# Scan's triangular inverses: substitution over 16x16 blocks, joined to 32x32 by small TensorE products

## The chip, the cores and the metric

One core of a Trainium2 chip. The metric is the device time of one execution in microseconds (us).

## The reference

A two-layer backbone over 512 latent and 256 context tokens of width 1024. Layer 0 mixes tokens by a gated MLP, layer 1 by a bidirectional RWKV-7 scan, and each layer ends in a mixture of experts. The change is in the scan of layer 1, which per direction and head (16 heads of 64) runs

```python
def _wkv_step(S, inp):
    r_t, w_t, k_t, v_t, a_t, b_t = inp
    sa = jnp.einsum('zbhvk,zbhk->zbhv', S, a_t)
    S = S * w_t[..., None, :] + sa[..., :, None] * b_t[..., None, :] + v_t[..., :, None] * k_t[..., None, :]
    return S, jnp.einsum('zbhvk,zbhk->zbhv', S, r_t)
```

first over the context, then over the latents. The kernel takes 64 tokens at a time. Within such a chunk the recurrence is a unit lower triangular system of 64x64 for each head, so each chunk and head needs the inverse of (I + L), with L strictly lower triangular.

## The kernel before

The scan stage (`Rwkv.wkv`) has 12 chunks in two directions, taken four at a time (two chunks of both directions) in six groups m = 0 to 5. Groups 0 and 1 are context, 2 to 5 latents. For a group there are three kinds of work:

- **prep_chunk** (four times a group) loads the chunk's keys and rates, scales them on VectorE (DVE) into `ZZ` and `BK`, lets TensorE (PE) form the attention blocks (`attend`, L1807) and transposes of `BK` (`turn`, L1828), and copies on ScalarE (ACT, L1816) the triangles L into `XT`.
- **invert** (once a group, for 4 chunks x 16 heads = 64 triangles, as 32 slots u of two) inverts. `gather` (L1852) transposes blocks so that each of the 128 partitions holds one 32x32 diagonal block. Forward substitution then runs on DVE: for each column j from 0 to 30 one product (L1856, into `subt`) and one subtraction (L1861, into `X`), each waiting for the one ahead. Two transposes bring the inverses back as `Dn` (L1881) and `Dt` (in the buffer of `Lp`, L1883). ACT places `Dt` in `XT` (`put`, L1865). PE then joins pairs of 32x32 to 64x64: `left` (L1896), an ACT copy with the sign turned (L1911), `right` (L1902), and an ACT copy into `XT` (L1916), all in two halves of 16 slots.
- **scan_step** (four a group) runs `read` (L1943), `solve` with the inverse (L1948), `update` (L1953) and, for latents, `outputs` (L1960, L1963) on PE; DVE (L1997) and GpSimd (POOL, L1998) bring the state on. Finished latents go through `finish` (DVE, and a transpose on PE, L2043).

The order on every engine is fixed when the program is built. Each `add` gives the planner (`Plan.run`) a step with an assumed cost, what it reads and what it writes. The planner takes the step that can start first by these costs, with the due times of `DUE` inside a small window. Buffers are rings: `X`, `Lp` and `Dn` have one each, the PSUM banks `p` three. Where the planner expects PE to stand idle ahead of a step that opens a bank, `Plan.fill` (L1146) issues products of the identity into that bank, about 0.8 of the expected idle time at 0.222 us each, and one in any case for the rings `p` and `y`:

```python
n = int(min(gap, FILLMAX) * FILL / 0.222) if gap >= FILLMIN else 0
for _ in range(max(n, XF if b.ring in XR else 0)):
    nc.tensor.matmul(q[:, 0:128], self.ident, self.ident, start=True, stop=True)
```

These fillers are real instructions: at run time they take their time whether or not PE would have waited. One f32 matmul is two records of the trace.

Of the kernel before, what the change touches and what calls it, by code (L numbers as in the profile page):

```python
# [17 lines left out]
P = 128  # L18
# [305 lines left out]
class Moe:  # L324
# [654 lines left out]
    def overflow(self, ep, ps, after):  # L979
# [5 lines left out]
        with tc.For_i(0, nv) as i:  # L985
# [57 lines left out]
            for g in after.groups:  # L1043
# [156 lines left out]
class Rwkv:  # L1200
# [474 lines left out]
    def consts(self, cp):  # L1675
        k = self.k
        nc = k.nc

        self.maskR = cp.tile([P, C], F32, name="maskR")
        self.maskY = [cp.tile([P, C], F32, name=f"maskY{z}") for z in range(2)]  # L1680
        for t, s in ((self.maskR, -1), (self.maskY[1], 1)):
            for h in range(2):
                nc.gpsimd.iota(t[64 * h:64 * h + 64, :], pattern=[[1, C]], base=0, channel_multiplier=s,
                               allow_small_or_imprecise_dtypes=True)
        nc.vector.tensor_scalar(self.maskY[0], self.maskR, 0.0, None, op0=ALU.is_ge)
        nc.vector.tensor_scalar(self.maskY[1], self.maskY[1], 63.0, None, op0=ALU.is_le)
# [146 lines left out]
    def invert(self, m):  # L1833


        add, nc = self.plan.add, self.k.nc
        self.plan.tag = "invert", 2 * m, 0
        g = m % 2
        XT = self.XT[:, g].rearrange("p c j t -> p (c j) t")
        Lk = [("L", g, i, n, p) for i in range(4) for n in range(2) for p in range(2)]  # L1840
        Lp, X, Dn, Dt = (self.buf(n, [P, 32, 32]) for n in ("Lp", "X", "Dn", "Lp"))

        def eye():
            nc.gpsimd.memset(X.t, 0.0)
# [26 lines left out]
        add("POOL", 1.8, eye, w=[(X, 0), (X, 1)])  # L1871
        add("DVE", 1.14, gather, r=Lk, w=[(Lp, 0)])
        for j in range(31):
            for e, (eng, w, a, b) in enumerate((("DVE", nc.vector, 0, min(j + 1, SPLIT)), ("POOL", nc.gpsimd, SPLIT, j + 1))):
                if a < b:
                    n = (31 - j) * (b - a)
                    c = 0.17 + n * 0.0021 if e else 0.07 + n / 960.0
                    t = self.buf(("subt", "subp")[e], [P, n], bufs=2)
                    add(eng, c, lambda w=w, t=t, j=j, a=a, b=b: times(w, t, j, a, b), r=[(X, e), (Lp, 0)], w=[t])
                    add(eng, c, lambda w=w, t=t, j=j, a=a, b=b: minus(w, t, j, a, b), r=[t], w=[(X, e)])  # L1880
        add("DVE", 1.14, lambda: nc.vector.transpose(Dn.t.rearrange("p u s -> p s u"), X.t.rearrange("p t s -> p s t")),  # L1881
            r=[(X, 0), (X, 1)], w=[(Dn, "1")])
        add("DVE", 1.14, lambda: nc.vector.transpose(Dt.t.rearrange("p u t -> p t u"), X.t), r=[(X, 0), (X, 1)], w=[Dt])  # L1883

        def put(b):
            add("ACT", 0.95, lambda: place(b), r=[Dt], w=[("XT", g, "diag", b)])

        for hf in range(2):
            us = range(16 * hf, 16 * hf + 16)
            q, q2 = self.bank([P, 16, 32]), self.bank([P, 16, 32])  # L1890
# [8 lines left out]
            def right(q=q2, us=us):  # L1899
                for u in us:  # L1900
                    for a, b in zip(fst, snd):
                        nc.tensor.matmul(q.t[a, u - us[0], :], Dn.t[b, u, :], XT[b, u, 32:64], start=True, stop=True,  # L1902
                                         tile_position=(b.start, a.start))

            self.plan.tag = "invert", 2 * m, 1
            add("PE", 0.9, left, r=[(Dn, "1")] + Lk, w=[q])
            if hf == 0:
                for b in (1, 3):
                    put(b)
            for p in range(2):  # L1910
                add("ACT", 0.48, lambda q=q, b=snd[p], us=us: nc.scalar.activation(Dn.t[b, us[0]:us[0] + 16, :], q.t[b], AF.Copy,  # L1911
                                                                                  scale=-1.0),
                    r=[q, (Dn, "1")], w=[(Dn, hf, p)])
            add("PE", 1.45, right, r=[(Dn, hf, 0), (Dn, hf, 1), ("XT", g, "diag", 1), ("XT", g, "diag", 3)], w=[q2])
            for p in range(2):
                add("ACT", 0.48, lambda q=q2, a=fst[p], us=us: nc.scalar.copy(XT[a, us[0]:us[0] + 16, 32:64], q.t[a]), r=[q2],  # L1916
                    w=[("XT", g, "off", hf, p)])
        for b in (0, 2):
            put(b)
        add("POOL", 1.8, blank, r=[(Lp, 0)], w=[("XT", g, "zero")])  # L1920

    def scan_step(self, h, z, c):
        add, nc = self.plan.add, self.k.nc
# [6 lines left out]
        s = self.sets.pop((z, c))  # L1930
        g, i = self.slot[z, c]
        Ti = self.XT[:, g, i]
        XTk = ([("XT", g, "off", i // 2, p) for p in range(2)] + [("XT", g, "diag", b) for b in range(4)] +
               [("XT", g, "zero")] + [("L", g, i, n, p) for n in range(2) for p in range(2)])
        SV = Buf(f"SV{z}", lambda: [self.sp.tile([P, KD, C], F32, name=f"SV{q}{z}", bufs=1) for q in range(2)], LATE)
        R, U, Sn, Y = self.bank([P, KD, C], "s3"), self.bank([P, KD, C], "s3"), self.bank([P, KD, C], "sn"), \
# [329 lines left out]
```

## Time and profile before

| | us |
|---|---|
| median of 3 runs (2615.51 to 2632.64) | 2625.8 |
| profiled execution | 2626.88 |
| its span | 2625.1 |
| scan stage in it, first gather to last write | 1554 to 2030 |
| share of the span that PE is busy | 91% |
| share that DVE is busy | 41% |
| share that ACT is busy | 28% |

Times in rows are us from the span's start. "Busy" of PE counts fillers too. [...]

### The profile page before, as it was taken

The page shows a single profiled execution, that of the slowest core. Times are in us where ns is not written, and L with a number is a line of the kernel's source. Part 1 is how long each engine was busy: PE and PEld are TensorE (multiplying, and loading weights), DVE is VectorE, ACT ScalarE, POOL GpSimd, SP SyncE. Part 2 cuts the span into 40 slices and gives each one's busy share as a digit, 9 for nine tenths or more (in the row PEclk, how much of TensorE's full clock was granted, in tenths as well). Part 3 has the DMA queues.
Part 4 walks back from the last instruction along what each step waited for, and adds up shares of the span by engine and source line. Part 5 has one row for each costly group of instructions (what it writes and reads, how often), then busy time and mean ns, then how long its engine had stood idle before and what let it go on. Part 6 is the DMA issues. An engine that isn't in the chain of part 4 may idle for free. (4 is left out here: it accounts for less than half of the span.)

```text
span 2625.1 us, 38933 instructions
## 1 busy us (share of the span) xinstructions
PE 2386.7 (91%) x15574; PEld 1514.6 (58%) x15574; DVE 1087.0 (41%) x2007; ACT 723.0 (28%) x1226; POOL 346.3 (13%) x306
## 2 busy tenths in 40 slices
PE   6999999997999999979979899889888799999985
PEld 2878997774334333346745488878787543333332
DVE  4334334444132111177655364887887511211113
ACT  3222213331000000036654345566544210000001
POOL 0000000003332222200012111211222110000000
PEclk8999999997999999988988699889999899999998
DMA  7135316558999999962256564533335699999995
GB/s 251 57 128 184 121 65 204 189 207 341 409 421 395 407 404 395 382 257 87 74 169 176 144 181 117 114 90 96 89 80 147 246 396 420 421 418 414 418 417 226
DMA packets 280077, 640.24 MB, mean 244 GB/s; under 512 B 131084, under 2 KB 156940, under 8 KB 229460
## 3 DMA queue, kind: packets, MB, share of 16 engines
q1 hardware_dynamic: 266548, 608.69, 63.0%
q0 software_dynamic: 11904, 23.77, 2.4%
q10 hardware_dynamic: 1440, 5.24, 0.5%
q8 instruction: 124, 2.03, 0.3%
q14 instruction: 61, 0.50, 0.1%
HBM read 580.65 MB, written 76.02 MB: 250 GB/s over the span
## 5 line engine op out<-in xcount | busy, mean ns | idle before, releaser
L935 PE MATMUL gu_ps<-e_raw,xT 128*64 128x512 f32 (+1 forms) x2048 | 587.4, 598 | 15.4 <-DMA e_raw<-moe_w_up 12.2
L935 PEld LDWEIGHTS gu_ps<-e_raw,xT 128*64 128x64 f32 (+1 forms) x2048 | 209.9, 149 | 372.7 <-issue 322.1
L891 PE MATMUL o_ps<-e_raw,hT 128*64 128x512 f32 (+1 forms) x1024 | 297.7, 603 | 5.0 <-ACT hT L867 5.0
L976 DVE TENSOR_TENSOR h_e<-gu_ps,h_e 128x512 f32<-128x512 f32 x39 | 27.0, 692 | 468.1 <-PE gu_ps L935 468.1
L891 PEld LDWEIGHTS o_ps<-e_raw,hT 128*64 128x64 f32 (+1 forms) x1024 | 104.7, 149 | 158.6 <-issue 144.4
L975 ACT ACTIVATE h_e<-gu_ps 128x512 f32<-128x512 f32 x39 | 23.3, 597 | 562.9 <-PE gu_ps L935 545.5
L1146 PE MATMUL p<-ident 128*128 128x128 f32 x892 | 139.9, 300 | 9.2 <-ACT BKt L1831 5.2
L1146 PEld LDWEIGHTS p<-ident 128*128 128x128 f32 x892 | 118.1, 204 | 21.7 <-ACT BKt L1831 7.2
L867 ACT COPY hT<-eT_ps 128x512 f32<-128x512 f32 x39 | 22.9, 586 | 355.6 <-PE eT_ps L861 355.6
L896 DVE SCALAR_TENSOR_TENSOR yo<-o_ps,wslot,gt_e 128x512 f32<-128x512 f32 x40 | 30.0, 751 | 182.2 <-issue 128.8
L826 POOL DMA_INDIRECT ybuf<-yo,idx x37 | 37.3, 1007 | 460.8 <-DVE yo L896 453.7
L73 PE MATMUL u_ps<-hh,w_hi 128*128 128x384 f32 x256 | 90.5, 353 | 4.9 <-ACT w_hi L66 4.9
L896 DVE SCALAR_TENSOR_TENSOR yo<-o_ps,wslot,gt2B 128x512 f32<-128x512 f32 x38 | 28.5, 750 | 158.2 <-PE o_ps L891 156.7
L812 POOL DMA_INDIRECT xg<-hbuf,idx x39 | 41.4, 1061 | 383.7 <-PE eT_ps L861 308.8
L74 PE MATMUL u_ps<-hl,w_hi 128*128 128x384 f32 x256 | 87.6, 342 | 0.0
L75 PE MATMUL u_ps<-hh,w_lo 128*128 128x384 f32 x256 | 86.3, 342 | 0.8 <-DVE w_lo L67 0.8
L67 DVE TENSOR_TENSOR w_lo<-w_raw,w_hi 128x1024 fp32r<-128x1024 f32 x56 | 67.9, 1222 | 38.1 <-ACT w_hi L66 37.4
L123 PE MATMUL ada_ps<-w_raw,cstat 128*32 128x512 f32 x384 | 62.8, 630 | 21.3 <-DMA w_raw<-ada_w 21.0
L73 PE MATMUL v_ps<-w_hi,hh 128*128 128x512 f32 x192 | 75.6, 406 | 3.9 <-ACT w_hi L66 3.9
L75 PE MATMUL v_ps<-w_hi,hl 128*128 128x512 f32 x192 | 75.7, 394 | 0.0
L74 PE MATMUL o_ps<-w_lo,gh 128*128 128x512 f32 x192 | 75.5, 395 | 0.0
L74 PE MATMUL v_ps<-w_lo,hh 128*128 128x512 f32 x192 | 75.5, 395 | 0.0
(562 smaller groups left out, 4415.1 us busy)
## 6 DMA issues: line engine op xcount, KB each, us to landing
e_raw<-moe_w_gate SPq DMA_DIRECT2D x128, 1024.0 KB, 19.8
e_raw<-moe_w_up SPq DMA_DIRECT2D x128, 1024.0 KB, 20.1
e_raw<-moe_w_down SPq DMA_DIRECT2D x128, 1024.0 KB, 19.8
w_raw<-ada_w SPq DMA_DIRECT2D x96, 512.0 KB, 6.4
w_raw<-ga_w_in SPq DMA_DIRECT2D x32, 512.0 KB, 6.5
Td<-c_st SPq DMA_DIRECT2D x64, 192.0 KB, 3.2
T<-Td SPq DMA_DIRECT2D x24, 512.0 KB, 4.9
ybuf<-zero_rows SPq DMA_DIRECT2D x20, 512.0 KB, 5.3
```

The source lines that it names most:

```text
L67: k.nc.vector.tensor_tensor(lo, src, hi.bitcast(F32), op=ALU.subtract)
L73: mm(out, a[0], b[0], start=start, stop=False)
L74: mm(out, a[0], b[1], start=False, stop=False)
L75: mm(out, a[1], b[0], start=False, stop=stop)
L123: nc.tensor.matmul(q[32 * g:32 * g + 32, :], k.cstat[:, j, :], w, start=(j < 4), stop=(j >= 4), tile_position=(0, 32 * g))
L812: k.nc.gpsimd.indirect_dma_start(out=xg[:], out_offset=None, in_=self.hbuf[:, :], in_offset=bass.IndirectOffsetOnAxis(ap=self.idx[:, 1, b: ...
L826: st = self.k.nc.gpsimd.indirect_dma_start(out=self.ybuf[:, :], out_offset=bass.IndirectOffsetOnAxis(ap=self.idx[:, 0, b:b + 1], axis=0), ...
L891: mm(o[hf][rows], hT[i][:, c, rows], self.raw[r, 4 + c // 2][:, f], start=c == 0, stop=c == 3)
L896: stt(yo[:, half(hf)], o[hf], self.wslot[:, u:u + 1], g[:, half(hf)], op0=ALU.mult, op1=ALU.mult)
L935: mm(q[gu][rows], xT[i][:, kk, rows], self.raw[r, 2 * gu + kk // 4][:, f], start=kk == 0, stop=kk == KD - 1)
L976: nc.vector.tensor_tensor(hv, u, hv, op=ALU.mult)
L1146: nc.tensor.matmul(q[:, 0:128], self.ident, self.ident, start=True, stop=True)
```

## The change

The diagonal blocks that DVE inverts become 16x16. One partition holds two of them (the two diagonal quarters of its 32x32 block), and one instruction works on both by a four-dimensional view, for columns 0 to 14. `X` and `Lp` get a row more (33 x 32), so that the two quarters lie a constant step apart. PE then joins 16x16 to 32x32 for each slot: `mid` multiplies the block with the inverse, ACT takes the result with a mask and the sign (`lower` is 0 or -1) into `Q` (in `X`'s buffer), `mid_n` makes the missing quarter of `Dn`, which DVE adds to it, and `mid_t` the missing quarter of `Dt`, which ACT places in `XT` (`between`). `left` and `right` are as before, but `left` now waits for the two additions and `right` for `between`. Some assumed costs are set anew (transposes 1.9 for 1.14, ACT copies 0.58 for 0.48, `left` 1.3 for 0.9).

```diff
-        def times(eng, t, j, a, b):
-            nr, nco = 31 - j, b - a
-            eng.tensor_tensor(t.t.rearrange("p (a b) -> p a b", a=nr), Lp.t[:, j + 1:, j:j + 1].to_broadcast([P, nr, nco]),
-                              X.t[:, j:j + 1, a:b].to_broadcast([P, nr, nco]), op=ALU.mult)
+        def times(t, j):
+            nr, nco = 15 - j, j + 1
+            nc.vector.tensor_tensor(
+                view(t, j), blocks(Lp)[:, :, 32 * (j + 1) + j:32 * 15 + j + 1:32][:, :, :, None].to_broadcast([P, 2, nr, nco]),
+                blocks(X)[:, :, 32 * j:32 * j + nco][:, :, None, :].to_broadcast([P, 2, nr, nco]), op=ALU.mult)
...
-        add("DVE", 1.14, gather, r=Lk, w=[(Lp, 0)])
-        for j in range(31):
...
+        add("DVE", 1.9, gather, r=Lk, w=[(Lp, 0)])
+        for j in range(15):
+            n = 2 * (15 - j) * (j + 1)
+            t = self.buf("subt", [P, n], bufs=2)
+            add("DVE", 0.12 + n / 960.0, lambda t=t, j=j: times(t, j), r=[X, (Lp, 0)], w=[t])
+            add("DVE", 0.12 + n / 960.0, lambda t=t, j=j: minus(t, j), r=[t], w=[X])
...
+        def mid(us):
+            for u in us:
+                for b in range(4):
+                    a = block(b)[0]
+                    nc.tensor.matmul(q1.t[a, u, :], XT[a, u, 0:32], Dn.t[a, u, 0:16], start=True, stop=True,
+                                     tile_position=(32 * b, 32 * b))
+        def mid_t(us):
+            for u in us:
+                for b in range(4):
+                    a = block(b)[0]
+                    nc.tensor.matmul(q2.t[32 * b:32 * b + 16, u, :], Q()[a, u, :], Dt.t[a, u, 16:32], start=True, stop=True,
+                                     tile_position=(32 * b, 32 * b))
+        def mid_n(us):
+            for u in us:
+                for b in (0, 2):
+                    a = block(b)[0]
+                    nc.tensor.matmul(q3.t[a, u, :], Dt.t[a, u, :], Q()[a, u, :], start=True, stop=True,
+                                     tile_position=(32 * b, 32 * b))
...
+        for hf, us in enumerate(halves):
+            add("PE", 2.6, lambda us=us: mid(us), r=[(Dn, "1")] + Lk, w=[(q1, hf)])
+        add("ACT", 0.58, lambda: nc.scalar.activation(Q(), q1.t, AF.Copy, scale=self.lower[:, 0:1]), r=[(q1, 0), (q1, 1)], w=[X])
+        for hf, us in enumerate(halves):
+            add("PE", 1.3, lambda us=us: mid_n(us), r=[X, Dt], w=[(q3, hf)])
+        for b in (0, 2):
+            add("DVE", 0.69, lambda a=block(b)[0]: nc.vector.tensor_tensor(Dn.t[a, :, 0:16], Dn.t[a, :, 0:16], q3.t[a], op=ALU.add),
+                r=[(q3, 0), (q3, 1), (Dn, "1")], w=[(Dn, "a", b)])
+        for hf, us in enumerate(halves):
+            add("PE", 2.6, lambda us=us: mid_t(us), r=[X, Dt], w=[(q2, hf)])
+        def between(b):
...
+            add("ACT", 0.58, lambda: nc.scalar.copy(XT[a, :, o + 16:o + 32], q2.t[a]), r=[(q2, 0), (q2, 1), ("XT", g, "diag", b)],
+                w=[("XT", g, "16", b)])
...
-            add("PE", 0.9, left, r=[(Dn, "1")] + Lk, w=[q])
+            add("PE", 1.3, left, r=[(Dn, "a", 0), (Dn, "a", 2)] + Lk, w=[q])
```

The planner's order moves with it. On PE ahead of group 1's `left`, before (L1807 is `attend`, L1146 filler, L1828 `turn`, L1896 `left`, L1902 `right`):

```order
L1807 MATMUL p<-ZZ,BK 128x128 x8
L1146 MATMUL p<-ident 128x128 x6
L1807 MATMUL p<-ZZ,BK 128x128 x8
L1146 MATMUL p<-ident 128x128 x48
L1896 MATMUL p<-Dn,XT 32x32 x64
L1146 MATMUL p<-ident 128x128 x15
L1902 MATMUL p<-XT,Dn 32x32 x32
L1146 MATMUL p<-ident 128x128
```

and at the same place in the changed kernel (L1812 is `attend`, L1145 filler, L1905 `mid`, L1921 `mid_n`, L1913 `mid_t`, L1954 `left`, L1960 `right`):

```order
L1812 MATMUL p<-ZZ,BK 128x128 x8
L1145 MATMUL p<-ident 128x128 x3
L1905 MATMUL p<-Dn,XT 32x16 x64
L1145 MATMUL p<-ident 128x128
L1812 MATMUL p<-ZZ,BK 128x128 x8
L1905 MATMUL p<-Dn,XT 32x16 x64
L1145 MATMUL p<-ident 128x128 x4
L1921 MATMUL p<-X,Lp 32x16 x64
L1913 MATMUL p<-Lp,X 16x16 x128
L1145 MATMUL p<-ident 128x128
L1954 MATMUL p<-Dn,XT 32x32 x32
```

The run of 48 fillers is gone, and 320 small products stand between the attention blocks and `left`.

On PE in group 4 of the changed kernel, between the scan steps:

```order
L1812 MATMUL p<-ZZ,BK 128x128 x8
L1145 MATMUL p<-ident 128x128
L1921 MATMUL p<-X,Lp 32x16 x64
L1145 MATMUL p<-ident 128x128
L1913 MATMUL p<-Lp,X 16x16 x64
L1145 MATMUL p<-ident 128x128
L1812 MATMUL p<-ZZ,BK 128x128 x8
L1913 MATMUL p<-Lp,X 16x16 x64
L2005 MATMUL s_14223<-SV_13819,ZZ 64x64
```

The new products stand among `attend` and ahead of `read` (L2005), which wait behind them.

On DVE the two additions to `Dn` (L1935) stand ahead of the next group's work; in the changed kernel, with L1826 the mask of prep_chunk and L1790 its `BK`:

```order
L1826 TENSOR_TENSOR QY<-p,maskY_9394 128x4x64
L1935 TENSOR_TENSOR Dn<-Dn,p 32x32x16 x2
L1790 TENSOR_TENSOR BK<-T,E_13052 128x2x8x64
```

A `BK` that a `turn` on PE needs is queued behind additions that wait for PE's `mid_n`.

Over the whole program the order has 1920 new small matmuls on PE (768 `mid`, 384 `mid_n`, 768 `mid_t`) and 161 fewer fillers (363 for 524), 180 substitutions on DVE for 372, and 12 additions. From the first `attend` on, cut at each group's first `solve`, the fillers in a piece go from 61, 132, 78, 66, 54, 78, 55 to 64, 79, 60, 44, 40, 16, 60.

## Rows read from the trace of the kernel before
**Rows 1.** Busy time of the engines in the scan stage, cut about where each group's first `solve` starts: stretch, its length, busy time (and instructions) of PE, PE's weight loads, DVE, ACT and POOL, granted clock, share of the DMA engines, GB/s.

```profile
1554.00:1615.00 61.00, 59.39 (x596) 51.10 (x596) 33.83 (x76) 23.39 (x40) 14.96 (x21) 0.94 0.37 120
1615.00:1706.00 91.00, 83.45 (x1176) 74.94 (x1170) 72.43 (x148) 54.13 (x117) 15.96 (x19) 0.92 0.53 117
1706.00:1776.00 70.00, 62.83 (x1025) 56.10 (x1018) 58.96 (x125) 42.13 (x85) 12.07 (x15) 0.90 0.37 85
1776.00:1844.00 68.00, 62.02 (x1196) 55.28 (x1196) 51.08 (x94) 43.94 (x88) 14.97 (x17) 0.95 0.45 106
1844.00:1911.00 67.00, 58.90 (x1146) 52.48 (x1141) 48.49 (x103) 38.89 (x78) 13.76 (x15) 0.95 0.28 73
1911.00:1974.00 63.00, 55.27 (x1110) 50.26 (x1103) 52.98 (x129) 28.78 (x48) 13.30 (x12) 0.90 0.36 98
1974.00:2030.00 56.00, 49.38 (x722) 44.19 (x721) 46.00 (x90) 24.49 (x43) 17.77 (x16) 0.93 0.52 142
sum 476.00, PE 431.24 PEld 384.34 DVE 363.77 ACT 255.75 POOL 102.80; mean PE 61.61 PEld 54.91 DVE 51.97 ACT 36.54 POOL 14.69
```

**Rows 2.** Groups of instructions in the stage (1540 to 2035): line, engine, operation, shapes, count, busy us, mean ns of one, idle time ahead of them and what ended it.

```profile
L1146 PE MATMUL p<-ident 128*128 128x128 f32 x846 | 131.4, 300 | 8.7 <-ACT BKt L1831 4.8 <-DVE BK L2047 1.5 <-ACT XT L1816 0.8
...
L1861 DVE TENSOR_TENSOR X<-X,subt 128x31 f32<-128x31 f32 (+15 forms) x186 | 73.1, 393 | 5.0
L1856 DVE TENSOR_TENSOR subt<-Lp,X 128x31 f32<-128x31 f32 (+15 forms) x186 | 70.2, 377 | 5.3
...
L1997 DVE TENSOR_TENSOR S<-sn,S 128x512 f32<-128x512 f32 x24 | 16.4, 683 | 4.3 <-PE sn L1953 3.7 <-issue 0.3 <-PE y L1960 0.2
L1902 PE MATMUL p<-XT,Dn 32*32 32x32 f32 x768 | 15.7, 195 | 1.6 <-ACT Dn L1911 1.6
...
L1911 ACT ACTIVATE Dn<-p 32x512 f32<-32x512 f32 x24 | 14.1, 589 | 21.0 <-PE p L1896 20.6
```

**Rows 3.** The same view as rows 1, for the stretches of the stage in which DVE is busiest.

```profile
1640.00:1690.00 50.00, 44.84 (x527) 39.89 (x527) 47.71 (x102) 27.85 (x64) 10.68 (x12) 0.93 0.71 153
1700.00:1730.00 30.00, 26.08 (x518) 23.19 (x517) 27.30 (x56) 21.10 (x40) 8.56 (x10) 0.96 0.22 56
1770.00:1810.00 40.00, 36.89 (x773) 33.20 (x772) 37.84 (x78) 24.34 (x48) 8.68 (x11) 0.91 0.32 82
1840.00:1880.00 40.00, 36.65 (x802) 32.54 (x799) 37.61 (x83) 22.92 (x45) 10.73 (x13) 0.96 0.41 107
1910.00:1960.00 50.00, 44.59 (x846) 40.20 (x842) 46.96 (x120) 20.50 (x37) 10.99 (x10) 0.95 0.29 78
sum 210.00, PE 189.06 PEld 169.03 DVE 197.42 ACT 116.71 POOL 49.63; mean PE 37.81 PEld 33.81 DVE 39.48 ACT 23.34 POOL 9.93
```

**Rows 4.** What PE waited for from 1554 to 2030: tile and line that waited, what released it, us in total, times, longest.

```profile
PE p L2043 <- DVE kk L2039: 7.8, 5, 2.2
PE p L1828 <- DVE BK L1785: 6.4, 5, 2.1
PE s L1948 <- ACT rhs L1974: 5.6, 5, 2.1
PE p L1146 <- ACT BKt L1831: 4.8, 5, 2.0
```

**Rows 5.** DVE's substitution by size, columns as in rows 2, stage from 1550 to 1980.

```profile
L1856 DVE TENSOR_TENSOR subt<-Lp,X 128x135 f32<-128x135 f32 x12 | 3.6, 298 | 0.4
...
L1856 DVE TENSOR_TENSOR subt<-Lp,X 128x112 f32<-128x112 f32 x12 | 3.3, 275 | 0.4
...
L1856 DVE TENSOR_TENSOR subt<-Lp,X 128x31 f32<-128x31 f32 x12 | 3.2, 266 | 0.7
```

**Rows 6.** PE in order of time at five places of the stage: start, us to the end of the last, line, operation, rows x columns of the weights, shape of what is moved, records. The step from one row's start to the next is what a row costs PE; its own us hold the last record's way out as well.

```profile
1602.15 1.10 PE L1807 MATMUL p<-ZZ,BK 64*128 64x64 f32 x8
1603.18 0.49 PE L1146 MATMUL p<-ident 128*128 128x128 f32 x2
...
1694.65 3.13 PE L1896 MATMUL p<-Dn,XT 32*32 32x32 f32 x128 [1.71 <-DVE Dn L1881]
...
1703.40 1.20 PE L1902 MATMUL p<-XT,Dn 32*32 32x32 f32 x64
1704.53 0.49 PE L1146 MATMUL p<-ident 128*128 128x128 f32 x2
...
1819.29 1.16 PE L1807 MATMUL p<-ZZ,BK 64*128 64x128 f32 x16
1820.38 0.49 PE L1146 MATMUL p<-ident 128*128 128x128 f32 x2
...
1826.73 3.84 PE L1146 MATMUL p<-ident 128*128 128x128 f32 x32
1830.50 1.16 PE L1807 MATMUL p<-ZZ,BK 64*128 64x128 f32 x16
```

**Rows 7.** The same view at two places ahead of the stage where outputs go to four column groups of the array: L123 takes the four in turn, L390 does four matmuls on one before it goes to the next.

```profile
30.82 1.99 PE L123 MATMUL ada_ps<-w_raw,cstat 128*32 128x512 f32 x12 [0.26 <-DVE mod L130]
...
408.25 1.45 PE L390 MATMUL shift_ps<-mod,ident 128*32 128x2 f32 x32
409.63 1.09 PE L54 MATMUL bc_ps<-ident,shift_dif 128*128 128x128 f32 x8
```

**Rows 8.** The group of L123 in the page's list of costliest groups (whole program; columns as in rows 2).

```profile
L123 PE MATMUL ada_ps<-w_raw,cstat 128*32 128x512 f32 x384 | 62.8, 630 | 21.3 <-DMA w_raw<-ada_w 21.0
```

More of the change, by code (lines that the diff above doesn't have):

```diff
@@ L1840, in invert @@
         Lk = [("L", g, i, n, p) for i in range(4) for n in range(2) for p in range(2)]
-        Lp, X, Dn, Dt = (self.buf(n, [P, 32, 32]) for n in ("Lp", "X", "Dn", "Lp"))
+        Lp, X, Dn, Dt = (self.buf(n, [P, w, 32]) for n, w in (("Lp", 33), ("X", 33), ("Dn", 32), ("Lp", 33)))
+        q1, q2, q3 = (self.bank([P, 32, 16]) for _ in range(3))
         def eye():
@@ L1869, in blank @@
                 nc.gpsimd.memset(XT[64 * p + 32:64 * p + 64, :, 0:32], 0.0)
-        add("POOL", 1.8, eye, w=[(X, 0), (X, 1)])
-        add("DVE", 1.14, gather, r=Lk, w=[(Lp, 0)])
-        for j in range(31):
[L1874 to L1880, printed above, removed]
@@ L1881, in invert @@
-        add("DVE", 1.14, lambda: nc.vector.transpose(Dn.t.rearrange("p u s -> p s u"), X.t.rearrange("p t s -> p s t")),
-            r=[(X, 0), (X, 1)], w=[(Dn, "1")])
-        add("DVE", 1.14, lambda: nc.vector.transpose(Dt.t.rearrange("p u t -> p t u"), X.t), r=[(X, 0), (X, 1)], w=[Dt])
-        def put(b):
-            add("ACT", 0.95, lambda: place(b), r=[Dt], w=[("XT", g, "diag", b)])
+        add("POOL", 1.8, eye, w=[X])
+        add("DVE", 1.9, gather, r=Lk, w=[(Lp, 0)])
[4 more added lines that the diff above has]
+            add("DVE", 0.12 + n / 960.0, lambda t=t, j=j: minus(t, j), r=[t], w=[X])
@@ new lines, in invert @@
+        add("DVE", 1.9, lambda: nc.vector.transpose(Dn.t.rearrange("p u s -> p s u"), X.t[:, 0:32].rearrange("p t s -> p s t")),
+            r=[X], w=[(Dn, "1")])
+        add("DVE", 1.9, lambda: nc.vector.transpose(Dt.t[:, 0:32].rearrange("p u t -> p t u"), X.t[:, 0:32]), r=[X], w=[Dt])
+        def put(b):
+            add("ACT", 0.95, lambda: place(b), r=[Dt, X], w=[("XT", g, "diag", b)])
+        def mid(us):
[4 more added lines that the diff above has]
+                                     tile_position=(32 * b, 32 * b))
@@ new lines, in mid_t @@
+        def mid_t(us):
+            for u in us:
+                for b in range(4):
+                    a = block(b)[0]
[7 more added lines that the diff above has]
+                                     tile_position=(32 * b, 32 * b))
@@ new lines, in Q @@
+        def Q():
+            return X.t.rearrange("p a b -> p (a b)")[:, 0:512].rearrange("p (u c) -> p u c", u=32)
+        halves = [range(16 * hf, 16 * hf + 16) for hf in range(2)]
+        for hf, us in enumerate(halves):
[3 more added lines that the diff above has]
+            add("PE", 1.3, lambda us=us: mid_n(us), r=[X, Dt], w=[(q3, hf)])
@@ new lines, in invert @@
+        for b in (0, 2):
[4 more added lines that the diff above has]
+        def between(b):
+            a = slice(32 * b, 32 * b + 16)
+            o = block(b)[1].start
+            add("ACT", 0.58, lambda: nc.scalar.copy(XT[a, :, o + 16:o + 32], q2.t[a]), r=[(q2, 0), (q2, 1), ("XT", g, "diag", b)],
+                w=[("XT", g, "16", b)])
@@ L1897, in left, with right @@
                                          tile_position=(a.start, b.start))
-            def right(q=q2, us=us):
+            def right(q=qr, us=us):
                 for u in us:
@@ L1919, in invert @@
             put(b)
-        add("POOL", 1.8, blank, r=[(Lp, 0)], w=[("XT", g, "zero")])
+        for b in (0, 2):
+            between(b)
+        add("POOL", 1.8, blank, r=[X], w=[("XT", g, "zero")])
     def scan_step(self, h, z, c):
@@ L1932, in scan_step @@
         Ti = self.XT[:, g, i]
-        XTk = ([("XT", g, "off", i // 2, p) for p in range(2)] + [("XT", g, "diag", b) for b in range(4)] +
+        XTk = ([("XT", g, "off", i // 2, p) for p in range(2)] + [("XT", g, x, b) for b in range(4) for x in ("diag", "16")] +
                [("XT", g, "zero")] + [("L", g, i, n, p) for n in range(2) for p in range(2)])
```

31 lines of the change are left out of this document (20 added, 11 removed).

## The prediction

> **What bounds the kernel now.** The change touches only the scan stage, so I read stretches of that stage and not the shares of the whole span. First, busy time by group [rows 1]: of 476 us PE is busy 431.2, DVE 363.8, ACT 255.8. By that PE looks full, with 44.8 us idle. Second, the groups of instructions [rows 2]: 846 records, 131.4 us, of PE's busy time are fillers, the products of the identity that the planner puts where it expects PE to wait. They stand in the queue and take their time whether PE waits or not. So PE's stream of instructions, fillers with it, sets the pace, and a chain that gets shorter on another engine gains nothing where the new order has as much on PE. Third, where PE still waits [rows 3, 4]: in five stretches of together 210 us DVE is busy for 197.4, and there PE is idle for 210 - 189.1 = 20.9 us; by releaser the waits are DVE's `finish` (7.8), DVE's `BK` (6.4) and ACT's copies (5.6, 4.8). So DVE paces the stage in part, and its substitution (73.1 + 70.2 = 143.3 us, rows 2) is the largest thing it does there. What is to be seen: an engine with too much to do in stretches, beside an engine kept full on purpose. The change takes from the first and gives to the second.
>
> **DVE.** Removed are 372 substitutions, 143.3 us. The 180 new ones work on 30, 56, 78, 96, 110, 120, 126, 128 elements and back down. The old forms of 31, 112 and 135 elements took 266, 275 and 298 ns [rows 5], so I price the new ones between 0.22 and 0.30: about 4.0 us for the 15 products of an inversion, as much for the subtractions, 8.0 us an inversion, 48 in all. Should the four-dimensional view make each cost 0.39, the mean of the old subtractions, it is 70. Added are 12 additions that read a PSUM bank, 512 elements in 32 partitions; the nearest row is L1997, which reads 512 from PSUM in 683 ns [rows 2]: 8.2 us. The idle time between dependent instructions (5.0 + 5.3 us for 372) halves to about 5. Net for DVE: -143.3 + 48 + 8.2 - 5 = about -92 us (-70 with the dear price). None of it goes straight into the sum: only what PE waits for it counts.
>
> **PE, fillers.** 161 are gone. Most come out of long runs; there 16 fillers (32 records) cost 1830.50 - 1826.73 = 3.77 us, 0.236 each [rows 6]. That is -38.0 us. A group of fillers costs about 0.1 us more than its count (0.33 from the start of a single one to the next row), and the new order has 18 groups more: +1.8. If each removed filler is worth the stage's mean (131.4 us over 423, rows 2), it is -50.
>
> **PE, small products.** The trace has no product of four 32x32 tiles in turn, so I bound it. `right`, which alternates two tiles, does 32 matmuls in 1704.53 - 1703.40 = 1.13 us, 35 ns each [rows 6]. At that price 1920 cost 67 us, the upper bound without the clock. That tiles run at once shows in `attend`: on one half of the array's rows, four matmuls (8 records) step on after 1.03 us, on both halves eight matmuls of twice the columns after 1.09 [rows 6]. That four can, shows in L123, whose 12 records go to four column groups in 1.99 us although one takes 0.63 us (12 x 0.63 = 7.6, so 3.8 at once) [rows 7, 8]. I therefore take half of 35 for `mid` and `mid_t`, which alternate four tiles, and 35 for `mid_n`, which alternates two: 1536 x 17.5 + 384 x 35 = 26.9 + 13.4 = 40.3 us. If the 16-column weights of `mid_t` halve its price again, it is 33.6, the lower bound. Sum for PE's stream: +40.3 - 38.0 + 1.8 = +4.1 us, between 33.6 - 50 + 1.8 = -15 and 67 - 38 + 1.8 = +31.
>
> The plan assumes 40 ns for each of these products (2.6 us for 64), so on the chip PE will be through them early; that is good for the chain and leaves PE to wait for what the plan hid behind them.
>
> **Waits.** The DVE waits in the five busy stretches are 20.9 us of PE idle time at most [rows 3]. `turn` waiting for `BK` and `finish` waiting for its last products are queued behind substitutions there; with 15 us less of these a group I let three quarters go: -15. What is late next is ACT: waits for its copies, 10.4 us in rows 4, stay. ACT gains 30 instructions of about 0.59 us (L1911, rows 2), 18 us over six groups; ACT is busy 255.8 of 476 us, so other waits cover them, and if the cover were gone at the end of each inversion (two `between` ahead of `right`), that would be 2 x 0.59 x 6 = 7 us. New hand-overs stand on the inversion's path: `mid` to ACT to `mid_n`, and `mid_n` to DVE to `left`. On PE `mid_t` (4 us at 35 ns, 2.2 at 17.5) stands between `mid_n` and `left` and hides the two additions (1.4 us). On DVE a `BK` is queued behind additions that wait for PE; a `turn` then waits with it. I take 0.5 us an inversion, +3; bounds 0 and 12.
>
> **The rest.** POOL clears 32 columns more and fills a constant once; no DMA is added. At the end of the stage the last group's order has 60 fillers for 55, inside the sum above.
>
> **Sum.** 4.1 - 15 + 3 = -8 us. The profiled execution took 2626.9, 1.1 over the median of the three runs, and I keep to it: 2626.9 - 8 = 2619 us, 0.3% less. The change moves work from DVE to PE, and PE gets back in fillers what it gives in small products.
>
> **Rivals.** *DVE was the pace in truth, and the stage shortens (faster).* For: the run of 48 fillers ahead of `left` in group 1 marks a place where everything waited for the substitution, and PE still waited for the transposes after it ([rows 6], the 1.71 us at L1896); DVE's share in the five stretches is 94%. Against: PE's stream is as long as before. Its floor is that stream: if all 44.8 us of idle time went and the stream stayed at +4, the stage would take 476 - 41, the program 2586. With half of all idle time gone and the cheap stream (-15) it is 2626.9 - 22 - 15 = 2590. From 29 us of waits gone on, at my price of the products, this is over 1%.
>
> *The small products are dear and cool the clock (slower).* At 35 ns for all of them the sum rises by 67 - 40 = 27. [...] If the mean clock falls by 0.03, 6% more of the time is at half speed, which on 476 us costs 14. Together 2619 + 27 + 14 = 2660. It decides from about 30 ns a product on with the clock, and needs both for over 1%. Against: tiles overlap in every row at hand.
>
> *The tiles of `mid` and `mid_t` take turns on their bank (slower).* All four row tiles of these products write one PSUM bank. In L390, which does four matmuls on one column group before the next, a record of 32 weight columns steps on after (409.63 - 408.25) / 32 = 43 ns [rows 7]; with two records for each matmul and nothing side by side, 1536 cost 132 us for 27, and the program 2619 + 105 = 2724. Against: `right` has two row tiles that write one bank, and a record steps on after 18 ns (1.13 us / 64). [...]
>
> *The change doesn't do what it says*, in that the dear DVE price holds: then DVE still loses 70 us, and the sum moves by a few us of the -15. It has no chance of its own.
>
> **How the numbers follow.** My forecast's case (PE's stream about even, some waits gone, 2600 to 2652) gets 0.46, faster by the first rival 0.30, dear products 0.21, turns on the bank 0.03. 1% is about what a measurement of this kernel can tell from no change. So faster 0.30, same 0.46, slower 0.24. The range goes to 2588, about where all of PE's idle time would be gone, and to the 2660 of the dear products; it leaves out a cheap stream with no idle time at all, and the turns on the bank.
>
> **What would show it.** In the changed kernel's profile: the 180 substitutions at 45 to 55 us (over 70 is the dear price); 64 `mid` products stepping on after 1.1 us (2.2 is the dear price, 5.5 the turns); fillers down by some 300 records and 40 us; PE's busy time in the stage within 15 us of 431; PE's idle time there at 30 rather than 45, with the waits for L1785 and L2039 shorter and those for ACT the longest; a mean granted clock still between 0.90 and 0.95. I am wrong on the mechanism if PE's busy time falls by more than 25 us, or if PE's idle time does not fall although DVE loses 90 us.

## The result and the profile after

| | before | after |
|---|---|---|
| median, us | 2624.5 (4 runs, 2615.5 to 2632.6) | 2660.4 (4 runs, 2657.6 to 2668.6) |
| ratio, with its 95% interval | | 1.0146 [1.0122, 1.0170] |
| profiled execution, its span | 2626.9, 2625.1 | 2657.6, 2655.8 |
| scan stage, first gather to the start of the last product of `finish` | 474.3 | 509.6 |
| PE busy, idle in it | 429.5, 44.8 | 449.0, 60.6 |
| time at the granted clock 0.5 in it | 68.3 | 122.9 |
| PE's idle time put down to "issue" in it | 0 | 27.5 |

The change costs 1.5%, 35.9 us by the medians. In the profiles the stage is 35.3 us longer, and the rest of the program is not: 19.5 us of the 35.3 is busy time of PE, 15.8 us idle time. The last two lines of the table are the ones to explain. The granted clock is a share of full speed; its records in the two traces hold the values 1.0 and 0.5 alone (2297.2 and 310.5 us before, 2293.8 and 347.0 after), so a number between them is a mean over both.

Busy time by group after, with the columns of [rows 1], cut about where each group's first `solve` starts:

```profile
1554.00:1631.00 77.00, 69.68 (x1218) 59.93 (x1218) 16.60 (x32) 24.13 (x42) 13.70 (x20) 0.80 0.24 77
1631.00:1732.00 101.00, 84.68 (x1707) 74.87 (x1702) 67.41 (x137) 57.43 (x122) 13.98 (x17) 0.82 0.45 106
1732.00:1797.00 65.00, 60.56 (x1626) 54.73 (x1622) 34.58 (x60) 45.05 (x89) 12.56 (x15) 0.96 0.36 86
1797.00:1874.00 77.00, 66.33 (x1788) 58.97 (x1782) 43.99 (x87) 47.51 (x93) 14.36 (x16) 0.91 0.39 96
1874.00:1950.00 76.00, 67.44 (x1773) 60.22 (x1767) 40.66 (x79) 42.56 (x85) 15.80 (x17) 0.87 0.26 69
1950.00:2004.00 54.00, 46.01 (x1539) 40.76 (x1540) 34.29 (x78) 30.66 (x49) 13.80 (x12) 0.84 0.35 96
2004.00:2061.00 57.00, 51.76 (x818) 45.41 (x813) 47.53 (x98) 25.66 (x45) 16.58 (x16) 0.98 0.60 160
sum 507.00, PE 446.45 PEld 394.88 DVE 285.07 ACT 273.00 POOL 100.78; mean PE 63.78 PEld 56.41 DVE 40.72 ACT 39.00 POOL 14.40
```

DVE fell from 363.8 to 285.1 us, as the change means it to; it is busy for 67% of a stretch at most, but for the last one (83%, about as before). The granted clock, 0.90 to 0.95 in [rows 1], is 0.80 to 0.87 in four of the seven stretches.

Groups of instructions after, from 1540 to 2065, with the columns of [rows 2] (L1145 are the fillers, L1876 and L1870 the substitution, L1905 `mid`, L1913 `mid_t`, L1921 `mid_n`, L1960 `right`):

```profile
L1145 PE MATMUL p<-ident 128*128 128x128 f32 x534 | 102.2, 319 | 14.1 <-ACT XT L1821 6.5 <-ACT BKt L1836 4.0 <-DVE kk L2099 1.7
...
L1876 DVE TENSOR_TENSOR X<-X,subt 128x30 f32<-128x30 f32 (+7 forms) x90 | 27.1, 302 | 2.9
...
L1870 DVE TENSOR_TENSOR subt<-Lp,X 128x30 f32<-128x30 f32 (+7 forms) x90 | 25.9, 288 | 3.1
...
L1905 PE MATMUL p<-Dn,XT 32*32 32x16 f32 x1536 | 18.1, 182 | 6.2 <-issue 6.2
L1960 PE MATMUL p<-XT,Dn 32*32 32x32 f32 x768 | 18.0, 207 | 1.3 <-issue 1.3
...
L1913 PE MATMUL p<-Lp,X 32*16 32x16 f32 x1536 | 16.1, 181 | 13.3 <-issue 13.3
...
L1921 PE MATMUL p<-X,Lp 32*32 32x16 f32 x768 | 15.4, 183 | 2.3 <-issue 1.4 <-ACT X L1931 0.7
```

What PE waited for from 1554 to 2063, columns as in [rows 4]:

```profile
PE p L1913 <- issue: 13.3, 8, 2.5
PE p L1145 <- ACT XT L1821: 6.5, 6, 2.9
PE p L1905 <- issue: 6.2, 7, 1.6
PE sn L2015 <- ACT SV L2038: 4.1, 4, 1.3
PE p L1145 <- ACT BKt L1836: 4.0, 4, 2.0
PE sn L2015 <- DVE S L2059: 3.7, 3, 1.7
PE s L2005 <- issue: 3.3, 3, 1.4
PE p L2105 <- DVE kk L2101: 3.2, 3, 2.2
PE p L1833 <- DVE BK L1790: 2.1, 3, 1.2
```

The waits for DVE's `kk` and `BK` went from 7.8 and 6.4 to 3.2 and 2.1 us. Above them stands a releaser that [rows 4] did not have: "issue", an idle time for which the profile shows no wait at all. PE in order of time, group 0, columns as in [rows 6], shows where it comes:

```profile
1572.46 1.20 PE L1913 MATMUL p<-Lp,X 32*16 32x16 f32 x122
1576.14 1.25 PE L1913 MATMUL p<-Lp,X 32*16 32x16 f32 x128 [2.49 <-issue]
1579.88 0.23 PE L1913 MATMUL p<-Lp,X 32*16 32x16 f32 x3 [2.48 <-issue]
1580.04 0.80 PE L1145 MATMUL p<-ident 128*128 128x128 f32 x2
1580.77 1.92 PE L1954 MATMUL p<-Dn,XT 32*32 32x32 f32 x64
1582.62 0.80 PE L1145 MATMUL p<-ident 128*128 128x128 f32 x2
...
1701.20 1.04 PE L1905 MATMUL p<-Dn,XT 32*32 32x16 f32 x103
1703.22 0.39 PE L1905 MATMUL p<-Dn,XT 32*32 32x16 f32 x25 [0.99 <-issue]
```

Within a run the products are as fast as forecast: 128 records, 64 products, end after 1.25 us. Then PE stops for 2.5 us, and between two such stops stand 128 records. A record is a weight load and a matmul, so 128 of them are 256 instructions. The queue that carries instructions moved more, too (page, section 3: packets, MB, share; before it had 124 packets):

```profile
q8 instruction: 151, 2.47, 0.4%
```

A packet of it is 16,384 bytes (2.47 MB over 151). The 27 packets more go with 7,036 more instructions of PE (page, section 1: 19,092 matmul records and as many weight loads, for 15,574 of each), some 260 a packet. Around the stops above the packets start at 1566.13, 1570.00, 1573.88, 1577.26 and 1581.01, one every 3.4 to 3.9 us. The other thing to see is `left` at 1580.77: 64 records step on after 1.85 us, at a granted clock of 0.50, where `right` did as many in 1.13 at 1.00 [rows 6].

### The profile page after: what moved, and what is told of

It is laid out like the page before. It is cut to its first block, busy times and chain, and to the rows that moved or that the text cites. A ratio compares the mean times of both kernels' runs of the same rounds, so it can differ in the third digit from the quotient of the medians.

```text
span 2655.8 us, 45835 instructions
## 1 busy us (share of the span) xinstructions
PE 2399.1 (90%) x19092; PEld 1526.4 (57%) x19092; DVE 1011.9 (38%) x1828; ACT 741.9 (28%) x1256; POOL 345.5 (13%) x310
## 3 DMA queue, kind: packets, MB, share of 16 engines
q8 instruction: 151, 2.47, 0.4%
## 4 chain that ended last, share of the span: by engine, by line
PE 37%; DMA 18%; DVE 8%; ACT 4%; issue 3%; SPq 1%; POOL 1%; DVEq 0%; ACTq 0%; POOLq 0%
PE gu_ps L935 8%; DMA e_raw<-moe_w_up 8%; DMA e_raw<-moe_w_gate 5%; DMA e_raw<-moe_w_down 5%; PE o_ps L891 4%; PE p L1145 2%; PE p L1812 2%; PE eT_ps L861 1%; PE g_ps L1537 1%; PE v L73 1%; PE p_ps L73 1%; PE v L74 1%; PE v L75 1%; PE p_ps L74 1%; PE p_ps L75 1%
## 5 line engine op out<-in xcount | busy, mean ns | idle before, releaser
L1145 PE MATMUL p<-ident 128*128 128x128 f32 x586 | 112.0, 317 | 14.6 <-ACT XT L1821 6.5
L1145 PEld LDWEIGHTS p<-ident 128*128 128x128 f32 x586 | 85.6, 209 | 28.1 <-ACT XT L1821 7.7
L73 PE MATMUL u_ps<-hh,w_hi 128*128 128x384 f32 x256 | 91.0, 355 | 5.5 <-ACT w_hi L66 5.4
L75 PE MATMUL u_ps<-hh,w_lo 128*128 128x384 f32 x256 | 86.5, 342 | 0.9 <-DVE w_lo L67 0.9
L1823 DVE TENSOR_TENSOR ZZ<-p,maskR 64x256 f32<-64x256 f32 x96 | 40.3, 419 | 107.2 <-PE p L1812 78.2
L123 PE MATMUL ada_ps<-w_raw,cstat 128*32 128x512 f32 x384 | 61.5, 611 | 21.2 <-DMA w_raw<-ada_w 20.6
L73 PE MATMUL v_ps<-w_hi,hh 128*128 128x512 f32 x192 | 75.4, 405 | 4.4 <-ACT w_hi L66 4.4
L73 PE MATMUL o_ps<-w_hi,gh 128*128 128x512 f32 x192 | 75.4, 398 | 0.0
```

Source lines behind the costliest of these rows:

```text
L73: mm(out, a[0], b[0], start=start, stop=False)
L75: mm(out, a[1], b[0], start=False, stop=stop)
L123: nc.tensor.matmul(q[32 * g:32 * g + 32, :], k.cstat[:, j, :], w, start=(j < 4), stop=(j >= 4), tile_position=(0, 32 * g))
L1823: tt(s.t["ZZ"][b, js, 2 * p, :], q.t[b, :, iR, :], mR[b], op=ALU.mult), r=[q], w=[(s, "A", n, p)])
```

## Experiments

Theory A: PE gets its instructions in blocks of 256, one in some 3.6 us; small products use up a block in 1.2 us and PE starves; the clock falls because of it. Rivals are named at each run. The run times of the kernel before were 2623.7 us (19 runs), 2626.1 (17) and 2626.0 (17) beside the three series; ratios are to these.

The stage in each profile, from its first gather to the start of the last product of `finish`, in us; the time at 0.5 is summed from the records of the granted clock:

| run | stage | PE busy | PE idle | "issue" | at 0.5 |
|---|---|---|---|---|---|
| before | 474.3 | 429.5 | 44.8 | 0 | 68.3 |
| after | 509.6 | 449.0 | 60.6 | 27.5 | 122.9 |
| e1_midt_wide | 482.5 | 435.1 | 47.4 | 9.6 | 75.1 |
| e2_all_wide | 468.9 | 429.4 | 39.6 | 2.6 | 58.0 |
| e4_fill_wide | 509.4 | 451.6 | 57.8 | 24.6 | 143.4 |
| e6_all_narrow | 491.3 | 458.2 | 33.2 | 1.2 | 112.6 |
| e7_bf16 | 480.0 | 430.5 | 49.5 | 6.6 | 119.5 |
| e8_price | 527.6 | 464.1 | 63.5 | 29.7 | 170.7 |
| e9_warm | 524.4 | 479.9 | 44.5 | 11.2 | 102.4 |
| e10_bf16_all | 461.8 | 412.3 | 49.5 | 5.0 | 109.3 |
| e12_before_lr | 472.9 | 425.6 | 47.3 | 0 | 86.1 |

Each row is one execution. Those of e4 and e7 are the shortest of their kernels (2650.6 and 2621.3 us), that of e8 is the longest (2687.7), and that of e12 has the lowest mean clock of its twelve. The part ahead of the stage, which the edits hardly touch, took from 1541 to 1560 us, so the stages compare better than the profiled programs do.

### The products by few instructions

e1 replaces the products of `mid_t`, e2 those of `mid` and `mid_n` as well, so that e1 leaves out the quarter of `Dt` and e2 all three joining quarters. From e1:

```diff
         def mid_t(us):
-            for u in us:
-                for b in range(4):
-                    a = block(b)[0]
-                    nc.tensor.matmul(q2.t[32 * b:32 * b + 16, u, :], Q()[a, u, :], Dt.t[a, u, 16:32], start=True, stop=True,
-                                     tile_position=(32 * b, 32 * b))
+            wide(q2, us, X, Dt)
...
+        def wide(q, us, *ws):
+            o = q.t.rearrange("p a b -> p (a b)")[:, 16 * us[0]:16 * us[0] + 256]
+            for i, n in enumerate((256, 256, 128)):
+                w = ws[i % len(ws)].t.rearrange("p a b -> p (a b)")[:, 0:128]
+                nc.tensor.matmul(o[:, 0:n].rearrange("p (r c) -> p r c", c=64), w,
+                                 self.zero[:, None, :].to_broadcast([P, n // 64, 64]), start=True, stop=True)
```

> The 768 products of mid_t are replaced by wide products of zeros that take PE as long (per half two of 256 columns and one of 128, 1.1 us, 12 instructions for 256), so the quarter of Dt is left out; all else, and the planner's costs, as in the changed kernel. Theory A (PE's instructions arrive in blocks of 256, one about every 3.6 us, and a run of small products eats one in 1.1 us): the 13 us in which PE waits for nothing at mid_t go, and part of the time at the low clock; 2640 us (2632 to 2648). Theory B (the new order on PE is longer by itself, with as many us of work): no change, 2660 (2652 to 2668).

> All 1920 small products are replaced by wide products of zeros of the same PE time, so the three joining quarters are left out; DVE, ACT and the order's form as in the changed kernel. Theory A: PE's waits for nothing (27 us in the stage) all but go, the time at the low clock goes back to that of the kernel before, 2615 to 2628 us. Theory B: no change, 2660 (2652 to 2668). Theory C (the relief of DVE is worth much and the small products hid it): under 2600.

Measured: e1 2635.3 us (10 runs), ratio 1.0044 [1.0023, 1.0065]; e2 2614.4 (10 runs), 0.9955 [0.9934, 0.9976]. e1 lies inside what A expected, e2 0.6 us under it and above the 2600 of theory C. With products of the same forecast time made by a handful of instructions the kernel is faster than before by 0.45%, where the forecast for the change had 0.3%. So the loss is not in what the products compute, nor in the new hand-overs between engines, which e2 keeps.

### The rate by itself

e3 is the kernel before with three runs of products put ahead of all else, 512 of 16 columns, 512 of 64 and 256 of 128, on four 32x32 tiles in turn:

```diff
+        def run16():
+            for i in range(512):
+                a = slice(32 * (i % 4), 32 * (i % 4) + 32)
+                nc.tensor.matmul(q[a, 0:16], k.ident[a, 0:32], k.ident[a, 0:16], start=True, stop=True, tile_position=(a.start, a.start))
...
```

> The kernel before, with three long runs on PE at its start, on the identity: 512 small products on four tiles with 16 columns moved, 512 with 64, 256 with 128, fillers between. Theory A: after the first blocks each record costs about 28 ns whatever it moves (two instructions a record, 256 in 3.6 us), so the runs take about 28, 28 and 15 us. If the array is the limit: 8.5, 15 and 28 ns a record, so 9, 15 and 15 us.

PE in order of time (L2203 16 columns, L2208 64, L2213 128):

```profile
14.08 1.24 PE L2203 MATMUL rate_q<-ident 32*32 32x16 f32 x127
17.22 1.25 PE L2203 MATMUL rate_q<-ident 32*32 32x16 f32 x128 [1.89 <-issue]
21.23 1.91 PE L2203 MATMUL rate_q<-ident 32*32 32x16 f32 x128 [2.76 <-issue]
...
42.89 7.08 PE L2198 MATMUL rate_q<-ident 128*128 128x128 f32 x48
49.90 3.10 PE L2208 MATMUL rate_q<-ident 32*32 32x64 f32 x207
54.09 1.99 PE L2208 MATMUL rate_q<-ident 32*32 32x64 f32 x128 [1.09 <-issue]
57.54 1.99 PE L2208 MATMUL rate_q<-ident 32*32 32x64 f32 x128 [1.47 <-issue]
...
76.45 7.25 PE L2198 MATMUL rate_q<-ident 128*128 128x128 f32 x48
83.63 14.18 PE L2213 MATMUL rate_q<-ident 32*32 32x128 f32 x512
97.74 2.50 PE L2198 MATMUL rate_q<-ident 128*128 128x128 f32 x20
```

The 1,024 records take 28.8 us with 16 columns (28.1 ns each) and 26.6 with 64 (25.9 ns); the 512 with 128 columns take 14.1 us (27.6 ns) and never stop. That is A's forecast of 28, 28 and 15 us. With 16 and with 64 columns PE starves alike, at one block in some 3.6 us. The granted clock does not go alike in the three runs (columns as in [rows 1]):

```profile
14.00:43.20 29.20, 14.40 (x1027) 13.42 (x1026) 4.93 (x11) 1.23 (x2) 0.00 (x0) 0.58 0.11 39
49.80:77.00 27.20, 16.47 (x1029) 15.21 (x1028) 0.00 (x0) 0.00 (x0) 0.00 (x0) 0.99 0.02 5
83.50:98.00 14.50, 14.50 (x516) 14.18 (x516) 0.00 (x0) 0.00 (x0) 0.00 (x0) 1.00 0.02 5
```

With 16 columns it lay at 0.5 most of the time (mean 0.58), with 64 nearly always at 1.0 (mean 0.99), although PE stood idle for 10.7 of 27.2 us there, too (14.8 of 29.2 with 16 columns). So idle time alone is a poor account of the clock's fall, which speaks against the second half of theory A but does not settle it. The DMA engines were nearly free (0.11 and 0.02 of their time), so the blocks were not slow for other traffic. The next run takes up the clock.

### Few instructions, few rows

The products of e2, on 32 of the array's 128 rows (weights of 32x128 in the trace, where a filler's are 128x128; against e2):

```diff
-                w = ws[i % len(ws)].t.rearrange("p a b -> p (a b)")[:, 0:128]
+                w = ws[i % len(ws)].t.rearrange("p a b -> p (a b)")[0:32, 0:128]
...
-                                 self.zero[:, None, :].to_broadcast([P, n // 64, 64]), start=True, stop=True)
+                                 self.zero[0:32, None, :].to_broadcast([32, n // 64, 64]), start=True, stop=True,
+                                 tile_position=(0, 0))
```

> The changed kernel with its three kinds of small products (1,920 in all) replaced by three products of zeros for each half, 640 columns together, as in the run that replaced all of them, but with 32 of the 128 rows of the array at work: few instructions, a fourth of the array. It leaves out the joining quarters of the inverses. Theory A (TensorE's instruction supply starves it, and the granted clock falls because of the idle time that this makes): no idle time on issue to speak of, and the time of the run with all 128 rows, 2614 us (2606 to 2625). Rival D (products that use little of the array lower the granted clock by themselves): the clock is low for as long as in the changed kernel (126 us between 1545 and 2065, where the run with all rows had 58), and the time is 2630 to 2645 us.

Measured: 2646.4 us (8 runs), ratio 1.0061 [1.0043, 1.0080], 1.4 us above rival D's range and 21 above A's: D's direction and about its size. There is next to no "issue" (1.2 us), yet the time at 0.5 is 112.6 us in place of e2's 58.0, and PE's busy time 28.8 us more. If a stretch at 0.5 does half its work (an estimate from the records of L73 to L75, under "The sum of PE's stream" below), half of the additional 54.6 us is 27.3. One row each, e2 and then e6:

```profile
1546.00:2017.00 471.00, 431.45 (x6816) 379.03 (x6815) 291.39 (x581) 273.53 (x527) 99.53 (x114) 0.94 0.41 108
```

```profile
1555.00:2048.00 493.00, 459.83 (x6815) 398.37 (x6814) 289.40 (x579) 273.22 (x526) 99.71 (x114) 0.89 0.39 101
```

The instructions, DVE and ACT are the same; the clock and with it PE's busy time are not. Over all executions the program's mean granted clock is 0.946 to 0.953 in e2 (10) and 0.932 to 0.938 in e6 (8). So the products on 32 rows went with the lower clock (0.89 for 0.94 in the stage) with next to no starving.

### Half the instructions

```diff
-                    nc.tensor.matmul(q1.t[a, u, :], XT[a, u, 0:32], Dn.t[a, u, 0:16], start=True, stop=True,
+                    nc.tensor.matmul(q1.t[a, u, :], high(XT[a, u, 0:32]), high(Dn.t[a, u, 0:16]), start=True, stop=True,
...
```

`mid_t` and `mid_n` are edited alike. `high(x)` is `x.bitcast(mybir.dt.bfloat16)[:, 1:2 * n:2]` for n columns.

> The changed kernel with the upper 16 bits of each operand of the small products read as bfloat16: the same 1,920 products at the same places on the same tiles of the array, but one pass and two TensorE instructions each in place of two passes and four, so 3,840 instructions fewer. It leaves out the lower bits of the joining quarters. Theory A (instruction supply): replacing 768 products took 25 us and all 1,920 took 46 us, and half of the 7,680 instructions go here: 2632 us (2624 to 2642), idle time on issue under 10 us, where it was 27.5. Rival D (the number of small products and the little of the array that they use): no less idle, the clock as low, 2650 us or more.

Measured: 2630.0 us (10 runs), ratio 1.0019 [1.0000, 1.0038], as A expected by its count of instructions: "issue" falls from 27.5 to 6.6 us. A small product is one record in place of two (768 of `mid` for 1,536), and the stage has 8,518 records of PE for 10,436. D is half right: the time at 0.5 stays (119.5). Of the 29.6 us that the stage gets shorter, 18.5 are busy time; half of the products' own 40.3 us is 20.2. So this run takes away starving and passes at once, does not tell the one from the other, and leaves the clock's part.

### What did not help

e4 takes the same fillers as products of up to 512 columns, 134 matmuls fewer; e8 only tells the planner a higher price; e9 puts wide products between the small ones.

```diff
...
+                for _ in range(n // r):
+                    nc.tensor.matmul(q[:, 0:128 * r].rearrange("p (r c) -> p r c", c=128), self.ident,
+                                     self.ident[:, None, :].to_broadcast([P, r, 128]), start=True, stop=True)
...
```

> The changed kernel with its fillers in long runs as products of 512 columns (one for four), 134 matmuls fewer for the same PE time. Theory A: 536 PE instructions fewer of some 20000 in the stage, and not where the small products run: -2 to -8 us, 2655 (2648 to 2661). Theory B: no change, 2660.

```diff
-            add("PE", 2.6, lambda us=us: mid(us), r=[(Dn, "1")] + Lk, w=[(q1, hf)])
+            add("PE", 3.6, lambda us=us: mid(us), r=[(Dn, "1")] + Lk, w=[(q1, hf)])
...
```

> The changed kernel, complete, with the planner's prices for the small products raised to the supply rate read from the trace (256 TensorE instructions in 3.6 us): 3.6 for a half of mid and mid_t in place of 2.6, 1.8 for mid_n, left and right in place of 1.3 and 1.45. Theory A (instruction supply, whatever the order): the same instructions pass, so 2655 us (2645 to 2665). Rival E (the loss is the planner's, which put too much behind products that take longer than it was told): 2640 us or less.

```diff
         def mid(us):
+            warm(q1, us[0:16])
             for u in us:
+                if u == us[8]:
+                    warm(q1, us[8:16])
...
```

> The changed kernel, complete, with 640 columns of wide products (identity by identity, into columns that the small products write afterwards) put into each half of mid and mid_t: one product of 256 columns ahead, three of 128 in the middle. That is 24 x 5 x 0.236 = 28 us of TensorE work at full clock in stretches where TensorE stood idle on issue for about 20 us, with 96 x 4 more instructions. Theory A with the clock as part of the loss: idle time on issue falls by 10 us or more, the stretches at the low clock shrink from 126 to under 100 us, and the time falls to 2647 us (2638 to 2655). Rival F (the starved time alone is the loss, the clock costs nothing): 2660 us or more, since the added work only fills idle time and its own instructions cost 5 us of supply.

Measured: e4 2658.1 us (4 runs), 1.0134 [1.0092, 1.0177], not to be told from the change itself, and so no help between A and B. e8 2668.8 (4 runs), 1.0144 [1.0117, 1.0172]: 4 us above A's range and far above rival E's 2640. Its ratio is about the change's own, so dearer prices for the planner, and the order that they bring, win nothing back. e9 2667.9 (4 runs), 1.0174 [1.0131, 1.0217]: a miss for A, and a time that rival F named. "issue" fell by 16.3 us, as A had it, and the time at 0.5 by 20.5, to a little over A's 100, but PE's busy time rose by 30.9 and the stage by 14.8.

The trace of e9 shows why, and that F's reason does not follow from its time. Of the time at 0.5 that went, 16.3 us lay in PE's idle time and only 4.1 in its busy time (19.4 and 103.4 us in the change itself, 3.1 and 99.3 in e9). So the clock had some 2 us to give back, while the added products brought some 33 us of work, an estimate made as under "The sum of PE's stream" below. The work put into the gaps filled them here but cost more than it won; what the clock alone is worth is not read from this run.

### A version that beats both

> The changed kernel with the upper 16 bits of each operand read as bfloat16 in all five kinds of products of the inverses, left and right too; it leaves out the lower bits of the joining quarters and halves. Against the run with the three new kinds alone (2630 us): 768 products give back half of their instructions (1,536) and half of their passes. A (supply and pass time both count): 2630 less 768 x 8.7 ns = 6.7 us of stepping, less some 5 us of idle time on issue and of low clock: 2617 us (2608 to 2626), so 0.3% under the kernel before. D (the clock is set by how little of the array is used, and gets worse with one pass in place of two): the low clock grows by as much as the passes give: 2627 to 2640 us.

> The kernel before with left and right alone (768 products) on the upper 16 bits of their operands; it leaves out the lower bits of the joining halves. It shows what this edit brings where there are no small products. Before has no idle time on issue in the stage, so by A only the stepping goes, and part of it is filled by fillers: 2621 us (2614 to 2627). By D the clock falls and takes it back: 2626 to 2635 us.

The edit is that of e7, made in `left` and `right` too (e10), and there alone in the kernel before (e12). Measured: e10 2608.8 us (6 runs), ratio 0.9926 [0.9904, 0.9948]; e12 2618.9 (12 runs), 0.9967 [0.9948, 0.9985]. With one pass for all small products the changed kernel is 0.7% faster than before, and the edit to `left` and `right` is worth about 0.9% there, 0.3% in the kernel before. Both times lie in A's ranges and under D's. In the profile of e12 768 products at half of 35 ns should give 13.4 us, but the time at 0.5 is 17.8 us longer and only 3.9 us of busy time went. That is no sign for D: over all executions the clock of e12 (0.937 to 0.949, median 0.944) is that of the kernel before (0.939 to 0.947, the same median), and the profile fell on the lowest. e10 gives up the lower bits of the joined quarters and halves for this.

## Why the prediction was wrong

**DVE: right.** The substitutions take 53.0 us (45 to 55 forecast), 90 less than before, and DVE's busy time fell from 363.8 to 285.1, by 79, where the forecast came to 87 without the idle time between instructions.

**Fillers: right.** 312 records fewer in `p` (some 300 forecast). Their busy time fell by 29.2 us and not by 38: the 534 that are left cost 191 ns of busy time each, where the 846 before cost 155. The lower clock (a record takes 319 ns for 300) and the missing long runs both bear on that; no run parts them.

**Small products inside a block: right.** 17.5 ns for `mid` and `mid_t`, 64 in 1.1 us of stepping. The rival of turns on one bank, at 43 ns a record, is refuted by the row of `mid_t` (8 to 9 ns), and e3 shows more: its four row tiles write one bank, and a record of 128 columns steps on after 27.6 ns, where a filler's, on the whole array, takes 118 (3.77 us for 32, [rows 6]). With turns, at 118 ns each, its 512 records would take some 60 us, an estimate; they took 14.1.

**The sum of PE's stream: the step that failed.** "1536 x 17.5 + 384 x 35 = 40.3 us" priced each product by its stepping in a short run, and took the clock to stay between 0.90 and 0.95; it was 0.88 over the stage. Two terms were missing.
- *Instructions.* 1,920 products are 7,680 instructions, 30 blocks of 256 at some 3.6 us each. An inversion's 320 products need 5 blocks, 18 us of supply, for 6.7 us of work. PE starved for 27.5 us (e3 shows the rate by itself; in e1, e2 and e7, with fewer instructions, it is 9.6, 2.6 and 6.6). The forecast asked how fast the array takes small products, not how fast it gets them.
- *Clock.* 54.6 us more at 0.5, of which PE was busy in 39.3 (64.1 before, 103.4 after). e6 has as much low clock nearly without starving. The rival "dear and cool" had the cost of it at 14 us, for a mean clock lower by 0.03; no run shows that term, and the mean over the stage fell by 0.05, from 0.93 to 0.88.

With these two the 35.3 us come out. A record of L73 to L75 (128x512) steps on after 0.43 us at a granted clock of 0.50 (1595.20 to 1596.48) and 0.23 at 1.00 (1599.24 to 1599.92). I take from it that time at 0.5 does about half the work, an estimate: not every record slows down so (64 of `right` took 1.85 us at 0.50 for 1.13 at 1.00, and 128 of `mid_t` ended after 1.25 us at 0.50, as 122 did after 1.20 at 0.95). Counted so, PE's busy time holds 429.5 - 32.0 = 397.5 us of work at full clock before and 449.0 - 51.7 = 397.3 after, an estimate. The work in PE's stream was thus about even, as the forecast had it (+4.1). The low clock adds 39.3 / 2 = 19.6 us of busy time, starving adds 27.5 us of idle time, and other waits give back 11.7: together 35.4 us.

What lowered the clock is shown less well. From e2 to e6, where only the rows at work differ, the stage grows by 22.4 us and the program by 32.0 (in the profiles 9 us of it lie ahead of the stage, unexplained); from e6 to the change itself the stage grows by another 18.3, the program by 14. That split rests on e6 as a stand-in: it uses one strip of 32 rows by 128 columns, where the small products use four tiles of 32 by 32 in turn. How much of the low clock in the change itself is owed to the tiles and how much to the starving stays open.

**Waits: nearly right.** PE's waits for DVE in the stage fell from 25.4 to 14.3 us, 11 of the forecast 15, and ACT's are the longest but "issue". The line "+3 for new hand-overs" held no room for the rest. PE's idle time was to fall to 30 and rose to 60.6; less its "issue" it is 33.1. Idle time that does not fall although DVE's load does was the prediction's own sign of a wrong mechanism, and it came.

**The rivals.** "Dear and cool" named the time (2660) and half of the cause: its 27 us for dear products came, as starving and not as 35 ns on the array, so that it hit the time is luck in good part. e2 at 2614 us, beside 2619 forecast, is about the kernel that the forecast priced.

## What to carry to other kernels

In the long runs here a small f32 product cost its four instructions: 256 came in some 3.6 us (e3), 14 ns each, 56 ns a product, where the stepping is 17.5. Elsewhere read both from the trace of a long run and take the larger. A row of 64 products says nothing on 320: in e3 127 records of 16 columns and 207 of 64 passed ahead of the first stop, and a short run ends before it. And ask of work that goes to a corner of the array what the granted clock does to everything that stands behind it; in group 0 `left` and `right` paid 1.85 us at 0.50 for 1.13 at 1.00.

## What the hardware showed that was not expected

- PE's instructions came as packets of 16,384 bytes (151 after, 124 before), about 256 instructions each by the 128 matmul records and 128 weight loads between two stops. While PE starved, one came in 3.4 to 3.9 us (after, 1566.13 to 1581.01), each taking about 1 us itself (median 1.03). PE stood idle for them with 16 and 64 columns (14.8 and 10.7 us), not with 128 (e3).
- Four f32 tiles of 16 columns stepped on at 8 to 9 ns a record inside a block, at a granted clock of 1.00 (after, 1701.20: 103 records of `mid` in 1.04 us, the last one's way out of some 0.18 us included) as at 0.50 (1576.14: 128 of `mid_t` in 1.25 us).
- The clock stayed at 0.99 while PE starved between products of 64 columns, and fell to 0.58 with 16 columns at nearly the same rate of instructions (e3, 25.9 and 28.1 ns a record).
